# Residual and result kept channel-major outside a two-layer DiT backbone kernel, in place of transposes on TensorE

## The chip, the cores and the metric

One core of one Trainium2 chip runs the whole program. The metric is the device time of one execution in microseconds, as a median over runs.

## What is computed

A backbone of two layers works on 512 latent tokens `x` with 256 context tokens `ctx` ahead of them, each token with 1024 channels. Layer 0 mixes tokens by windowed attention, layer 1 by a gated linear recurrence (HGRN2). A channel mixer (ConvGLU) closes each layer. Every sub-layer normalises its input, scales and shifts it by vectors made from the conditioning, and adds its output, times a gate, to the stream. Cut to what matters here:

```python
for layer in range(DEPTH):                     # 2
    hx = rms_norm(x, norm1_g[layer]) * (1.0 + sc1) + sh1
    hc = rms_norm(ctx, norm1_g[layer]) * (1.0 + csc1) + csh1
    yx, yc = windowed_gqa(hx, hc, ...) if layer == 0 else hgrn2_bidir(hx, hc, ...)
    x = x + g1 * yx                            # the residual
    x = x + g2 * conv_glu(rms_norm(x, norm2_g[layer]) * (1.0 + sc2) + sh2, ...)
    if not last:
        ctx = ctx + cg1 * yc                   # and the same for the context
        ctx = ctx + cg2 * conv_glu(...)
return x                                       # (1, 512, 1024)
```

`x` has a batch of one and comes as 512 rows of 1024 channels; the result has the same form.

## The kernel before, in words

Everything inside the kernel is channel-major. The 1024 channels are 8 blocks (`d`) of 128 channels, a block lies on the 128 partitions, and tokens run along the free dimension. The stream is held as `self.xl` (128 x 8 x 512, latent) and `self.xc` (128 x 8 x 256, context). A matrix product takes weights (128 x 128) as the stationary operand and tokens as the moving one. Weights and activations are split into a high and a low fp32r part; each product is three (`wh` with high, `wh` with low, `wl` with high). ScalarE makes `wh` and VectorE `wl` (L118 and L119 in `load_w`) from the raw tile `wr` or `wd` that a transfer from the SP queue brought.

Outside, tokens are rows, so the kernel turns the data round at three places:

- `first_norm` loads `x` and `ctx` token-major (SP queue, at the start), normalises and transposes them for the first sub-layer. It keeps no copy of the raw stream.
- `attn_out` (L928 to L951) is the output projection of the attention. For each of four pairs `(dp, dp+4)` of channel blocks it loads the weights, and for each block of a pair it loads the stream's slice again, token-major, into `xs` by two transfers on ScalarE's queue (L937: 4 x 128 tokens of `x`, 256 KB; L938: 2 x 128 of `ctx`, 128 KB). Six transposes of 128 x 128 on TensorE (L941) put it into a PSUM tile `xT`, and two ScalarE copies (L943) move it to `xl` and `xc`. Then 48 products (8 input blocks, three parts, latent and context) fill the PSUM tile `ao`, and `add_gated` (VectorE, L955) adds `ao` times the gate to `xl` and `xc`. Behind each pair stand the squares of the new stream (`square_acc`, L552 and L554) and the operands `hs` of the channel mixer (`combos`, L382 to L404, L449 to L452). Two PSUM pools serve `xT` and two serve `ao`, in turn.
- `done1` (L1536 to L1556) is called for each channel block when its last down projection (`dn`, L177) has been added to the stream (L1116; L1111 for the last block, which is added in two halves of 256 tokens). It transposes the block back (L1551, four transposes into the PSUM tile `xo`; L1543, two for each half of the last block), copies `xo` to an SBUF tile `ost` or `osl` on ScalarE (L1552, L1544) and starts a transfer on the SP queue: one for each of three pairs of blocks (L1556, 512 KB), one for block 6 (L1554, 256 KB) and one for each half of block 7 (L1545, 128 KB).

The attention ends with `split_o`: the output `o` of the last group of heads, copied from the PSUM tile `pv` (L884), is split into `oh`, its high part by ScalarE (L893), its low one by VectorE (L894). `oh` is the moving operand of the output projection; its last two input blocks come from this last split.

The order of the instructions on each engine is set by a scheduler that simulates a timeline; weight loads and splits have a raised priority. An edit in one place can therefore move rows that it does not name.

Of the kernel before, what the change touches and what calls it, by code (L numbers as in the profile page):

```python
# [8 lines left out]
F32 = mybir.dt.float32  # L9
F32R = mybir.dt.float32r  # L10
BF16 = mybir.dt.bfloat16
AF = mybir.ActivationFunctionType
ALU = mybir.AluOpType
AX = mybir.AxisListType
PSUM = bass.MemoryType.PSUM

P = 128
D = 1024
KT = D // P
LAT = 512  # L20
CTX = 256
TOK = LAT + CTX
NQ = LAT // P
# [50 lines left out]
class Kernel:  # L74
    def __init__(self, tc, a, dbg=None):
        self.tc, self.nc, self.a, self.dbg = tc, tc.nc, a, dbg or {}
# [848 lines left out]
        es.close()  # L925
        return ohs[0]

    def attn_out(self, oh, hs, acc, tmp, pj, pp):  # L928
        nc, a = self.nc, self.a
        wout = a["attn_w_out"][0]  # L930
        for dp in range(KT // 2):
            w = self.load_w([self.wcols(wout, d * P, P) for d in (dp, dp + 4)])
            for j in range(2):
                d = dp + 4 * j
                xs = tmp.tile([P, 6, P], F32, tag="xs", name="xs")
                cs = slice(d * P, (d + 1) * P)
                nc.scalar.dma_start(out=xs[:, 0:4], in_=a["x"][0, :, cs].rearrange("(t p) c -> p t c", p=P))  # L937
                nc.scalar.dma_start(out=xs[:, 4:6], in_=a["ctx"][0, :, cs].rearrange("(t p) c -> p t c", p=P))  # L938
                pt = pp.tile([P, 1024], F32, tag="p2", name="xT")
                for i in range(6):  # L940
                    nc.tensor.transpose(pt[:, i * P:(i + 1) * P], xs[:, i], self.ident)  # L941
                for lo, hi, x in self.segs(False):
                    nc.scalar.activation(x[:, d], pt[:, lo:hi], AF.Copy)  # L943
                ps = pj.tile([P, 1024], F32, tag="pj", name="ao")
                self.mm_feat(w[j], KT, lambda k: (oh[:, 0, k], oh[:, 1, k]), self.spans(ps, FULL))
                self.add_gated(0, 2, d, ps, False)
            ops = self.combos(self.halves(0, 1, dp, 386, False, tmp, ("G", "nt")), dp, hs)
            for _ in range(2):
                next(ops)
            for d in (dp, dp + 4):  # L950
                self.square_acc(d, acc, False, tmp, first=(d == 0))  # L951
# [477 lines left out]
    def run(self, stop=99):  # L1429
        nc, a = self.nc, self.a  # L1430
# [10 lines left out]
        oh = self.attention(hn)  # L1441
# [17 lines left out]
        tmp = self.pool(es, "tmpA", 1)  # L1459
        acp = self.pool(es, "accA", 1)  # L1460
        acc = Rp.tile([P, TOK], F32, tag="acc", name="acc0")
        hs = [*(h1[:, i] for i in range(4)), h2[:, 0], h2[:, 1]]
        with ExitStack() as e2:
            pp, pj = (_Turn([self.pool(e2, f"{n}{i}", 1, PSUM) for i in range(2)]) for n in ("ppA", "pjA"))
            xsp = self.pool(e2, "xsp", 2)
            self.attn_out(oh, hs, acc, _Multi(tmp, xsp, ("xs",)), pj, pp)
        rs.close()
        if stop == 2:
            self.dump_x(); es.close(); hss.close(); hB.close(); top.close(); return
# [7 lines left out]
        gp = self.pool(es, "gpA", 5)  # L1477
# [27 lines left out]
        e2 = ExitStack()  # L1505
        sc = self.pool(e2, "sc", 2, PSUM)
        lv = self.pool(e2, "lv", 2, PSUM)
        pj = self.pool(e2, "pj", 2, PSUM)
        part = self.hgrn(hn2[0], R, accs[0], hb, pj, lv, sc)
# [3 lines left out]
        hs = [hs1[:, i] for i in range(8)]  # L1513
        ot = self.pool(es, "ot", 1)
        acc = Rp.tile([P, LAT], F32, tag="acc", name="acc2")
# [10 lines left out]
        tmp = self.pool(es, "tmpB", 2)  # L1526
        acp = self.pool(es, "accB", 1)
        gp = self.pool(es, "gpB", 9)
# [2 lines left out]
        bk = [self.pool(es, "bkB0", 4, PSUM), self.pool(es, "bkB1", 4, PSUM)]  # L1531
        bk = _Turn(bk, bk[:1] * 3)
        rows = self.row_factor(acc, True, tmp, bk, "ps", 512, R, -1.0)
        ost = {}

        def done1(d, bank, part=None):  # L1536

            if d == KT - 1:
                n = LAT // 2
                pt = bank("xo")  # L1540
                o = gp.tile([P, 2, P], F32, tag="g", name="osl")
                for i in range(2):
                    nc.tensor.transpose(pt[:, i * P:(i + 1) * P], self.xl[:, d, part * n + i * P:part * n + (i + 1) * P], self.ident)  # L1543
                nc.scalar.activation(o, pt[:, :n].rearrange("p (i c) -> p i c", c=P), AF.Copy)  # L1544
                nc.sync.dma_start(out=a["out"][0, part * n:part * n + n, d * P:(d + 1) * P].rearrange("(t p) c -> p t c", p=P), in_=o)  # L1545
                return
            if d % 2 == 0:
                ost[0] = gp.tile([P, NQ, 256], F32, tag="g", name="ost")
            pt = bank("xo")
            for i in range(NQ):  # L1550
                nc.tensor.transpose(pt[:, i * P:(i + 1) * P], self.xl[:, d, i * P:(i + 1) * P], self.ident)  # L1551
            nc.scalar.activation(ost[0][:, :, (d % 2) * P:(d % 2) * P + P], pt[:, :LAT].rearrange("p (i c) -> p i c", c=P), AF.Copy)  # L1552
            if d == KT - 2:
                nc.sync.dma_start(out=a["out"][0, :, d * P:(d + 1) * P].rearrange("(t p) c -> p t c", p=P), in_=ost[0][:, :, 0:P])  # L1554
            elif d % 2:
                nc.sync.dma_start(out=a["out"][0, :, (d - 1) * P:(d + 1) * P].rearrange("(t p) c -> p t c", p=P), in_=ost[0])  # L1556

        self.ffn(1, hs, R, rows, True, tmp, acp, bk, gp, done1)
        es.close()
        rs.close()  # L1560
# [8 lines left out]
class _Halves:  # L1569
# [5 lines left out]
    def tile(self, *a, **kw):  # L1575
        return self.parts.pop(0)
# [12 lines left out]
        return self.pools[-1].tile(*a, **kw)  # L1589


class _Multi:


    def __init__(self, p0, p1, tags):
        self.p0, self.p1, self.tags = p0, p1, tags

    def tile(self, shape, dt, tag=None, name=None, **kw):
        return (self.p1 if tag in self.tags else self.p0).tile(shape, dt, tag=tag, name=name, **kw)


_INS = ['x', 'c', 'ctx', 'c_ctx', 'ada_w', 'ada_b', 'norm1_g', 'norm2_g', 'attn_w_in', 'attn_w_out', 'attn_q_gain',
        'attn_k_gain', 'attn_sink', 'hgrn_w_in', 'hgrn_w_out', 'hgrn_o_gain', 'hgrn_lb_logits', 'ffn_w_up',
        'ffn_conv_w', 'ffn_conv_b', 'ffn_w_down']
# [18 lines left out]
```

## Time and profile before

| | before |
|---|---|
| median of 3 runs | 1773.47 us (1773.41 to 1774.19) |
| the profiled execution's own time | 1773.3 us |
| its span in the trace | 1771.5 us |
| granted TensorE clock, mean | 0.999 |
| TensorE busy | 1742.6 us, 98% of the span |
| VectorE, ScalarE, GpSimd busy | 1308.5, 833.6, 247.3 us |
| moved by DMA | 166.44 MB, mean 94 GB/s |

The span is the stretch between the first and the last record of the execution; its own time is the 1.8 us longer device time. Busy times of one engine count its instructions that overlap only once. The chain that the page shows is followed back from the last instruction: each piece is work, or a wait for what released it. TensorE (PE) overlaps the load of one weight tile (PEld) with the product before it.

### The profile page before, as it was taken

The numbers are of one execution on the slowest core, as the hardware profiler recorded it, in microseconds if no ns is written. First come the engines' busy times: TensorE is split into PE (matmuls) and PEld (weight loads), VectorE is DVE, ScalarE is ACT, GpSimd is POOL, SyncE is SP. The second block draws the span as 40 slices with busy tenths as digits, with TensorE's granted clock in tenths as the row PEclk, the third lists the DMA queues.
The fourth block names the chain that finished last, engine by engine and source line by source line (L and its number), as shares of the span: only waits on it lengthen the run. The fifth ranks groups of instructions, "written<-read, shape, count | busy, mean of one in ns | idle before, by whom it ended". The sixth has DMA issues, their size and how long they took to land.

```text
span 1771.5 us, 32299 instructions
## 1 busy us (share of the span) xinstructions
PE 1742.6 (98%) x13033; PEld 1528.3 (86%) x13033; DVE 1308.5 (74%) x2394; ACT 833.6 (47%) x1740; POOL 247.3 (14%) x232
## 2 busy tenths in 40 slices
PE   5999999999999999999999999999999999999998
PEld 4967775789889888999999889999897899999997
DVE  6576677477777776867867767777776699999984
ACT  4355556565534443534455333333333465565553
POOL 1133333200100110100100101111110001111110
PEclk9999999999999999999999999999999999999999
DMA  9351005133333343213114212121225423333311
GB/s 309 110 198 42 24 2 191 52 92 113 122 120 99 123 139 96 87 42 99 54 52 117 62 45 61 53 57 40 58 73 190 123 72 105 110 105 108 91 59 66
DMA packets 205188, 166.44 MB, mean 94 GB/s; under 512 B 5406, under 2 KB 199023, under 8 KB 199919
## 3 DMA queue, kind: packets, MB, share of 16 engines
q1 hardware_dynamic: 197376, 160.47, 29.5%
q10 hardware_dynamic: 7662, 3.92, 0.8%
q8 instruction: 102, 1.67, 0.4%
q14 instruction: 48, 0.39, 0.1%
HBM read 162.27 MB, written 2.10 MB: 93 GB/s over the span
## 4 chain that ended last, share of the span: by engine, by line
PE 96%; DMA 2%; DVE 1%; ACT 0%; issue 0%; POOL 0%; SPq 0%; ACTq 0%; DVEq 0%
PE dn L177 17%; PE pZ L195 17%; PE pV L195 8%; PE pf L177 8%; PE pY L195 4%; PE pjq L634 4%; PE pv L177 4%; PE ao L177 4%; PE pv L882 3%; PE pgate L177 3%; PE pq L177 3%; PE pt L872 3%; PE ada L316 2%; PE kv L634 2%; PE pd L969 2%; PE S L814 2%
## 5 line engine op out<-in xcount | busy, mean ns | idle before, releaser
L195 PE MATMUL pZ<-hs,wh 128*128 128x386 f32 (+1 forms) x1312 | 296.7, 314 | 0.0
L177 PE MATMUL dn<-g,wh 128*128 128x512 f32 (+1 forms) x1062 | 268.0, 356 | 0.0
L142 ACT ACTIVATE wh<-wr 128x512 fp32r<-128x512 f32 x246 | 153.7, 629 | 242.7 <-PE pZ L195 89.2
L118 ACT ACTIVATE wh<-wr 128x512 fp32r<-128x512 f32 (+2 forms) x204 | 120.2, 603 | 271.5 <-PE pf L177 82.1
L195 PEld LDWEIGHTS pZ<-hs,wh 128*128 128x128 f32 x1312 | 224.1, 189 | 14.8 <-ACT wh L142 5.9
L143 DVE TENSOR_TENSOR wl<-wr,wh 128x512 fp32r<-128x512 f32 x246 | 182.5, 746 | 35.8 <-ACT wh L142 31.6
L195 PE MATMUL pZ<-hs,wl 128*128 128x386 f32 (+1 forms) x656 | 204.7, 313 | 0.0
L177 PEld LDWEIGHTS dn<-g,wh 128*128 128x128 f32 x1062 | 174.7, 189 | 25.7 <-ACT g L1062 0.3
L119 DVE TENSOR_TENSOR wl<-wr,wh 128x512 fp32r<-128x512 f32 (+2 forms) x204 | 140.4, 695 | 74.3 <-ACT wh L118 65.1
L992 POOL TENSOR_TENSOR gg<-gg,R 128x772 f32<-128x772 f32 (+1 forms) x41 | 85.3, 2079 | 715.2 <-DVE gg L991 626.0
L177 PE MATMUL dn<-g,wl 128*128 128x512 f32 (+1 forms) x531 | 162.1, 355 | 0.0
L195 PE MATMUL pV<-hs,wh 128*128 128x386 f32 (+1 forms) x656 | 148.6, 313 | 0.0
L195 PEld LDWEIGHTS pZ<-hs,wl 128*128 128x128 f32 x656 | 123.4, 188 | 0.1
L177 PE MATMUL pf<-hn,wh 128*128 128x512 f32 (+1 forms) x512 | 117.7, 344 | 0.6 <-DVE gate L1160 0.6
L195 PEld LDWEIGHTS pV<-hs,wh 128*128 128x128 f32 x656 | 111.9, 189 | 1.3 <-issue 0.8
L195 PE MATMUL pV<-hs,wl 128*128 128x386 f32 (+1 forms) x328 | 102.2, 313 | 0.0
L177 PEld LDWEIGHTS dn<-g,wl 128*128 128x128 f32 x531 | 89.4, 188 | 14.2
L1116 DVE SCALAR_TENSOR_TENSOR xl<-dn,mod,xl 128x512 f32<-128x512 f32 x95 | 70.5, 745 | 29.6 <-PE dn L177 29.5
L177 PEld LDWEIGHTS pf<-hn,wh 128*128 128x128 f32 x512 | 79.4, 189 | 12.1 <-DVE gate L1160 0.8
L634 PE MATMUL pjq<-wh,hn 128*128 128x256 f32 x384 | 76.8, 289 | 0.0
L195 PE MATMUL pY<-hs,wh 128*128 128x386 f32 (+1 forms) x328 | 76.7, 314 | 0.0
L822 POOL TENSOR_SCALAR P<-P,r 128x512 f32<-128x512 f32 (+1 forms) x64 | 53.0, 832 | 95.8 <-DVE r L821 73.8
(321 smaller groups left out, 3895.9 us busy)
## 6 DMA issues: line engine op xcount, KB each, us to landing
wr<-in_ffn_w_up SPq DMA_DIRECT2D x88, 512.0 KB, 5.2
wada<-in_ada_w SPq DMA_DIRECT2D x40, 1024.0 KB, 5.0
wr<-in_hgrn_w_in SPq DMA_DIRECT2D x40, 512.0 KB, 5.1
ar<-in_ada_w SPq DMA_DIRECT2D x32, 256.0 KB, 7.0
wd<-in_ffn_w_down SPq DMA_DIRECT2D x16, 512.0 KB, 3.4
wr<-in_attn_w_in SPq DMA_DIRECT2D x6, 1024.0 KB, 8.5
wr<-in_ffn_w_down SPq DMA_DIRECT2D x12, 384.0 KB, 3.0
wr<-in_attn_w_out SPq DMA_DIRECT2D x8, 512.0 KB, 4.3
```

Source lines behind the costliest of these rows:

```text
L118: nc.scalar.activation(wh, src, AF.Copy)
L119: nc.vector.tensor_tensor(wl, src, f(wh), op=ALU.subtract)
L142: nc.scalar.activation(ops[i][0], src, AF.Copy)
L143: nc.vector.tensor_tensor(ops[i][1], src, f(ops[i][0]), op=ALU.subtract)
L177: nc.tensor.matmul(o, lhsT=wt, rhs=at[:, t0:t0 + o.shape[1]], start=(first and n == 0 and i == 0), stop=(last and n == len(ks) - 1 and i = ...
L195: self.nc.tensor.matmul(ps, lhsT=wt, rhs=at, start=(first and k == 0 and i == 0), stop=(k == nk - 1 and i == 2), skip_group_check=not first)
L634: nc.tensor.matmul(out, lhsT=x, rhs=y[:, wk], start=(start and k == 0 and j == 0), stop=(stop and k == KT - 1 and j == 2))
L822: nc.gpsimd.tensor_scalar(p[:, :n], p[:, :n], r[:, j:j + 1], 1.0, op0=ALU.mult, op1=ALU.mult)
L872: nc.tensor.transpose(pt[:, j * P:(j + 1) * P], pr[j][:, b * P:(b + 1) * P], self.ident)
L882: nc.tensor.matmul(pv[a * HD:(a + 1) * HD, 0:256], lhsT=V[:, tiles[b], g, :], rhs=pT[:, a * 256:(a + 1) * 256], start=(b == 0), stop=(b == ...
L992: times = lambda eng, o, x, y: eng.tensor_tensor(o, x, y, op=ALU.mult)
L1116: nc.vector.scalar_tensor_tensor(x[:, d], o, self.modc(l, v, 5, d), x[:, d], op0=ALU.mult, op1=ALU.add)
```

## The change

The host hands over the stream a second time, as `xT` (1024 x 512) and `ctxT` (1024 x 256), and takes the result as `out_0` of 1024 x 512, which it transposes back. In `attn_out` the transfers go straight to `self.xl` and `self.xc`, one of each per pair of blocks: four of 512 KB and four of 256 KB on ScalarE's queue (L934 after), with rows of 2 KB and 1 KB. The transposes, their PSUM tiles, the copies and `xs` are gone, and the PSUM banks that served them go to `ao`: four pools, `p0 p1 p2 p3 p2 p3 p2 p3` in turn over the eight blocks. `done1` is one transfer from `xl` for each block (L1531 after): seven of 256 KB, and two of 128 KB for the last block. `first_norm` is as before.

```diff
-    def attn_out(self, oh, hs, acc, tmp, pj, pp):
+    def attn_out(self, oh, hs, acc, tmp, pj):
...
             w = self.load_w([self.wcols(wout, d * P, P) for d in (dp, dp + 4)])
+            for x, src in ((self.xl, a["xT"]), (self.xc, a["ctxT"])):
+                nc.scalar.dma_start(out=x.rearrange("p (j d) t -> p j d t", j=2)[:, :, dp],
+                                    in_=src.rearrange("(j d p) t -> p j d t", j=2, p=P)[:, :, dp])
             for j in range(2):
                 d = dp + 4 * j
-                xs = tmp.tile([P, 6, P], F32, tag="xs", name="xs")
-                cs = slice(d * P, (d + 1) * P)
-                nc.scalar.dma_start(out=xs[:, 0:4], in_=a["x"][0, :, cs].rearrange("(t p) c -> p t c", p=P))
-                nc.scalar.dma_start(out=xs[:, 4:6], in_=a["ctx"][0, :, cs].rearrange("(t p) c -> p t c", p=P))
-                pt = pp.tile([P, 1024], F32, tag="p2", name="xT")
-                for i in range(6):
-                    nc.tensor.transpose(pt[:, i * P:(i + 1) * P], xs[:, i], self.ident)
-                for lo, hi, x in self.segs(False):
-                    nc.scalar.activation(x[:, d], pt[:, lo:hi], AF.Copy)
                 ps = pj.tile([P, 1024], F32, tag="pj", name="ao")
...
-            pp, pj = (_Turn([self.pool(e2, f"{n}{i}", 1, PSUM) for i in range(2)]) for n in ("ppA", "pjA"))
-            xsp = self.pool(e2, "xsp", 2)
-            self.attn_out(oh, hs, acc, _Multi(tmp, xsp, ("xs",)), pj, pp)
+            pj = [self.pool(e2, f"pjA{i}", 1, PSUM) for i in range(4)]
+            self.attn_out(oh, hs, acc, tmp, _Turn(pj + 2 * pj[2:]))
...
-            if d == KT - 1:
...
-                for i in range(2):
-                    nc.tensor.transpose(pt[:, i * P:(i + 1) * P], self.xl[:, d, part * n + i * P:part * n + (i + 1) * P], self.ident)
-                nc.scalar.activation(o, pt[:, :n].rearrange("p (i c) -> p i c", c=P), AF.Copy)
-                nc.sync.dma_start(out=a["out"][0, part * n:part * n + n, d * P:(d + 1) * P].rearrange("(t p) c -> p t c", p=P), in_=o)
-                return
...
-            for i in range(NQ):
-                nc.tensor.transpose(pt[:, i * P:(i + 1) * P], self.xl[:, d, i * P:(i + 1) * P], self.ident)
-            nc.scalar.activation(ost[0][:, :, (d % 2) * P:(d % 2) * P + P], pt[:, :LAT].rearrange("p (i c) -> p i c", c=P), AF.Copy)
...
+            c = slice(0, LAT) if part is None else slice(part * LAT // 2, (part + 1) * LAT // 2)
+            nc.sync.dma_start(out=a["out"][d * P:(d + 1) * P, c], in_=self.xl[:, d, c])
...
+    data["xT"] = np.ascontiguousarray(data["x"][0].T)
+    data["ctxT"] = np.ascontiguousarray(data["ctx"][0].T)
...
-    args["out"] = nc.dram_tensor("out_0", (1, LAT, D), F32, kind="ExternalOutput").ap()
+    args["out"] = nc.dram_tensor("out_0", (D, LAT), F32, kind="ExternalOutput").ap()
...
-    return r.results[0]["out_0"]
+    return np.ascontiguousarray(r.results[0]["out_0"].T)[None]
```

The scheduler's order differs at the end of the attention and in the tail behind the last up projection; elsewhere the engines' rows stand as before. (Numbers behind a name tell buffers apart and differ between the two programs; `oh_3949`, `xl_4232` and `xc_4250` are the same in both.)

TensorE where the attention's last value products `pv` meet the output projection, before:

```order
L177 MATMUL ao_4304<-oh_3949,wl_4281 128x512
L177 MATMUL ao_4304<-oh_3949,wl_4281 128x256
L882 MATMUL pv_4191<-pT_4197,V_917 64x256 x2
L941 MATMUL xT_4358<-cst_64,xs_4355 128x128 x4
L882 MATMUL pv_4191<-pT_4204,V_917 64x256 x2
L941 MATMUL xT_4358<-cst_64,xs_4355 128x128 x2
L177 MATMUL ao_4367<-oh_3949,wh_4284 128x512
```

The same place after:

```order
L177 MATMUL ao_4342<-oh_3949,wh_4281 128x512
L882 MATMUL pv_4191<-pT_4197,V_917 64x256 x2
L177 MATMUL ao_4342<-oh_3949,wh_4281 128x256
L882 MATMUL pv_4191<-pT_4204,V_917 64x256 x2
L177 MATMUL ao_4342<-oh_3949,wh_4281 128x512
L177 MATMUL ao_4342<-oh_3949,wh_4281 128x256
```

Where two transposes stood behind the last `pv`, 16 more products of the block `ao_4342` follow, and 15 of the block `ao_4496`, ahead of the first product that takes the last two input blocks of `oh`.

ScalarE behind the last copy of `o`, before (`y` of L383 are small norm factors):

```order
L884 ACTIVATE o_918<-pv_4191 128x2x128
L383 ACTIVATE y_4418<-mod0_123 128x2
L383 ACTIVATE y_4423<-mod0_123 128x2
L937 DMA xs_4531<-in_x 128x4x128
L893 ACTIVATE oh_3949<-o_918 128x768 x2
L938 DMA xs_4531<-in_ctx 128x2x128
L118 ACTIVATE wh_4452<-wr_4449 128x512
L118 ACTIVATE wh_4456<-wr_4449 128x512
L943 ACTIVATE xl_4232<-xT_4295 128x512
L943 ACTIVATE xc_4250<-xT_4295 128x256
```

After:

```order
L884 ACTIVATE o_918<-pv_4191 128x2x128
L934 DMA xc_4250<-in_ctxT 128x2x256
L118 ACTIVATE wh_4439<-wr_4424 128x512
L893 ACTIVATE oh_3949<-o_918 128x768 x2
L383 ACTIVATE y_4393<-mod0_123 128x2
L383 ACTIVATE y_4398<-mod0_123 128x2
L934 DMA xc_4250<-in_ctxT 128x2x256 x3
L118 ACTIVATE wh_4427<-wr_4424 128x512
L118 ACTIVATE wh_4431<-wr_4424 128x512
L934 DMA xl_4232<-in_xT 128x2x512 x4
L118 ACTIVATE wh_4583<-wr_4580 128x512
L382 ACTIVATE y_4393<-xl_4232,gs0_125 128x512
```

One weight split stands ahead of the `oh` splits now, the `xc` transfers around them, and the four `xl` transfers behind two more weight splits, where the copies from `xT` stood.

TensorE in the tail, at the first use of the last channel-mixer block `g` (`g_19318` before, `g_19226` after), before:

```order
L177 MATMUL dn_19446<-g_18944,wl_19439 128x512
L177 MATMUL dn_19446<-g_19131,wh_19438 128x512 x2
L177 MATMUL dn_19446<-g_19131,wl_19439 128x512
L177 MATMUL dn_19407<-g_19318,wh_19399 128x512
L177 MATMUL dn_19408<-g_19318,wh_19403 128x512
```

After:

```order
L177 MATMUL dn_19383<-g_18852,wl_19379 128x512
L177 MATMUL dn_19383<-g_19039,wh_19378 128x512 x2
L177 MATMUL dn_19383<-g_19039,wl_19379 128x512
L177 MATMUL dn_19416<-g_18852,wh_19408 128x512 x2
L177 MATMUL dn_19315<-g_19226,wh_19307 128x512
L177 MATMUL dn_19316<-g_19226,wh_19311 128x512
```

Ahead of that use TensorE has 27 `dn` products behind its last up product before, and 47 after; `dn_19383` is the sixth block of the last round, `dn_19446` was the third.

More of the change, by code (lines that the diff above doesn't have):

```diff
@@ L1533, in run @@
         rows = self.row_factor(acc, True, tmp, bk, "ps", 512, R, -1.0)
-        ost = {}
         def done1(d, bank, part=None):
-            if d == KT - 1:
-                n = LAT // 2
-                pt = bank("xo")
-                o = gp.tile([P, 2, P], F32, tag="g", name="osl")
-                for i in range(2):
-                    nc.tensor.transpose(pt[:, i * P:(i + 1) * P], self.xl[:, d, part * n + i * P:part * n + (i + 1) * P], self.ident)
-                nc.scalar.activation(o, pt[:, :n].rearrange("p (i c) -> p i c", c=P), AF.Copy)
-                nc.sync.dma_start(out=a["out"][0, part * n:part * n + n, d * P:(d + 1) * P].rearrange("(t p) c -> p t c", p=P), in_=o)
-                return
-            if d % 2 == 0:
-                ost[0] = gp.tile([P, NQ, 256], F32, tag="g", name="ost")
-            pt = bank("xo")
-            for i in range(NQ):
[L1551 to L1556, printed above, removed]
+            c = slice(0, LAT) if part is None else slice(part * LAT // 2, (part + 1) * LAT // 2)
+            nc.sync.dma_start(out=a["out"][d * P:(d + 1) * P, c], in_=self.xl[:, d, c])
         self.ffn(1, hs, R, rows, True, tmp, acp, bk, gp, done1)
@@ L1589, in tile @@
         return self.pools[-1].tile(*a, **kw)
[L1592 to L1599, printed above, removed]
 _INS = ['x', 'c', 'ctx', 'c_ctx', 'ada_w', 'ada_b', 'norm1_g', 'norm2_g', 'attn_w_in', 'attn_w_out', 'attn_q_gain',
```

## The prediction

> **What bounds the kernel now.** I read the page first, its busy shares and its chain by engine, then the chain piece by piece in the two stretches that the change touches, then the timeline of the other engines there.
>
> ```profile
> span 1771.5 us, 32299 instructions
> ...
> PE 1742.6 (98%) x13033; PEld 1528.3 (86%) x13033; DVE 1308.5 (74%) x2394; ACT 833.6 (47%) x1740; POOL 247.3 (14%) x232
> ...
> PE 96%; DMA 2%; DVE 1%; ACT 0%; issue 0%; POOL 0%; SPq 0%; ACTq 0%; DVEq 0%
> ```
>
> TensorE (PE) is busy 98% of the span and carries 96% of the chain that ended last. An edit that takes PE work away therefore gains that work's length, if nothing else becomes late. The profiled execution took 1773.3 us, 1.8 more than its span; the median of the three runs is 1773.47, so 0.2 is added to a time reckoned from the profile.
>
> The first stretch, the end of the attention with its output projection, in the windows view (length, then busy time of PE, weight loads, DVE, ACT and GpSimd, the granted clock, DMA share, GB/s), and PE's transposes there:
>
> ```profile
> 328.50:408.90 80.40, 80.28 (x489) 68.02 (x492) 49.13 (x93) 48.35 (x114) 2.70 (x16) 1.00 0.27 79
> ```
>
> ```profile
> L941 PE MATMUL xT<-cst,xs 128*128 128x128 f32 x48 | 6.8, 275 | 0.0
> ```
>
> PE has no idle time (80.28 of 80.40), DVE and ACT are busy for 61%, and the clock is at 1.00 with all 48 transposes inside. In the chain over 328 to 412 us (start, length, piece) the same transposes stand so:
>
> ```profile
> by line: PE ao L177 80.5%; DMA wr<-in_ffn_w_up 6.4%; PE xT L941 6.2%; PE pv L882 5.2%; PE pt L872 3.8%; ACT o L884 0.5%; SPq L96 0.4%; issue 0.2%; PE Sc L814 0.1%; PE Sc L817 0.1%
> ...
> 332.45 0.66 PE xT L941 x6
> ...
> 342.01 0.59 PE xT L941 x4
> 342.60 0.61 PE pv L882 x4
> 343.21 0.02 issue
> 343.23 0.39 ACT o L884
> 343.62 0.04 issue
> 343.67 10.76 PE ao L177 x60
> 354.43 0.87 PE xT L941 x8
> ...
> 400.44 8.44 PE ao L177 x48
> ```
>
> 6.2% of 84 us is 5.2 us of transposes on the path. Between 343.21 and 343.67 PE also waits 0.46 us for ScalarE to copy out the last attention output o. Then only projection products follow, 48 for each block of 128 channels, 0.176 us each.
>
> The second stretch is the tail, the chain over 1749 to 1772 us:
>
> ```profile
> by line: PE dn L177 59.5%; PE xo L1551 13.9%; ACT ost L1552 2.6%; ACTq L1619 1.2%; ACT osl L1544 1.2%; issue 0.1%
> ...
> 1752.12 0.57 PE xo L1551 x4
> ...
> 1765.37 0.45 PE xo L1551 x4
> 1765.82 0.02 issue
> 1765.85 0.60 ACT ost L1552
> 1766.44 0.28 ACT osl L1544
> 1766.72 0.28 ACTq L1619
> ```
>
> The xo transposes take 13.9% of 23 us, 3.2 us in seven groups; the last group (0.45) stands behind the last down product, the other six (2.75) stand between products. Behind the last product, at 1765.37, the timeline has:
>
> ```profile
> 1765.41 0.48 DVE L1111 SCALAR_TENSOR_TENSOR xl<-dn,mod,xl 128x256 f32<-128x256 f32 x1 [0.58 <-PE dn L177]
> ```
>
> ```profile
> 1767.19 0.92 SPq L1545 DMA_DIRECT2D out<-osl  x2
> ```
>
> The last add is done at 1765.89, but the last of two output transfers is issued only around 1767.65 (its half of the 0.92), after transposes and copies. From there to the span's end are 1771.5 - 1767.65 = 3.85 us.
>
> **Part 1, the residual loads.** Removed: 48 transposes on PE, 5.2 us, all on the path; the ACT copies (16, of 0.4 to 0.6 us) and half of the 16 ACT-queue transfers were beside PE, worth nothing. In the new order PE has 31 ao products between the last pv and the first that needs the last channel pair of oh (16 of one block, 15 of the next). They take 31 x 0.176 = 5.5 us and have to cover the chain that makes oh:
>
> ```profile
> 344.89 1.83 DVE L894 TENSOR_TENSOR oh<-o,oh 128x768 fp32r<-128x768 f32 x2 [1.23 <-ACT oh L893]
> ```
>
> ```profile
> 346.75 1.15 ACT L118 ACTIVATE wh<-wr 128x512 fp32r<-128x512 f32 x2 [1.16 <-DVE oh L894]
> 347.81 0.58 ACT L943 ACTIVATE xl<-xT 128x512 f32<-128x512 f32 x1
> ```
>
> Before, oh is complete at 344.89 + 1.83 = 346.72, 3.5 us after the last pv. One weight split (half of 1.15) is moved ahead of it, so about 4.1 us against 5.5 of cover: the wait of 0.46 for o goes and no new one comes, with 1.4 us to spare. If that cover were gone the price is 4.1 less what is left of 5.5. Against this, the new order cuts the last pv products apart with ao rows. Such a switch costs about 0.15: four xT beside pv took 0.59, where half of the eight in 0.87 is 0.44. Three more switches cost 0.45. Net: 5.2 + 0.46 - 0.45 = **-5.2 us**.
>
> The loads come late, and that is where this part could fail. The four xl transfers stand on ScalarE behind two weight splits that end, by the rows above, about where ScalarE used to copy xl (347.8). What can be said of their landing:
>
> ```profile
> wr<-in_attn_w_in SPq DMA_DIRECT2D x6, 1024.0 KB, 8.5
> ...
> xs<-in_x ACTq DMA_DIRECT2D x8, 256.0 KB, 2.9
> out<-ost SPq DMA_DIRECT2D x3, 512.0 KB, 2.9
> ```
>
> The new 512 KB ones lie between 2.9 and 8.5. The nearest row is 2.9 (same queue or same size), but with 3.1 MB in one burst at 79/0.27 = 293 GB/s (10.7 us for all) I take 5 for the first. The first reader is DVE's gated add:
>
> ```profile
> 351.17 0.75 DVE L955 SCALAR_TENSOR_TENSOR xl<-ao,mod,xl 128x512 f32<-128x512 f32 x1 [0.51 <-PE ao L177]
> ```
>
> So DVE is held until about 353, 2 us (0 to 5) longer than before. Queued behind it on DVE are the weight splits of later blocks, on ScalarE the norm steps that read xl. PE needs neither soon. The first two blocks have PSUM banks that no later block of this stage takes (four pools, before two), so the first bank wanted again is the third block's, two blocks (2 x 8.44 us) after that block's end, and the split weights held up behind the add are those of the third pair of channels, about 20 us on. The delay costs 0; with a landing at 8.5 and one block of cover (8.44) it would cost next to nothing still.
>
> **Part 2, the output.** Removed between products: six xo groups, **-2.75 us**. A further wait goes in the tail:
>
> ```profile
> PEld dn L177 <- ACT g L1062: 0.3, 1, 0.3
> ```
>
> Before, PE ran 27 products between its last up product and the first that needs the last g; the new order has 47, 20 x 0.23 = 4.6 us more cover, so this small wait goes: **-0.2** (0 to 0.5). Behind the last product: before 1767.65 - 1765.37 = 2.28 us to the last issue; now the add alone (0.04 + 0.48) and about 0.15 to the issue, 0.67: **-1.6 us**. Last, the transfers: nine instead of six, all in the last six microseconds of products; 2.1 MB at 293 GB/s are 7.2 us, of which some 5.6 lie beside the products and the rest inside the 3.85 of the last transfer. I take **+0.2** (0 to +1.5).
>
> The sum is -5.2 - 2.75 - 0.2 - 1.6 + 0.2 = -9.6: 1773.3 - 9.6 = 1763.7 for the profiled execution, 1763.9 as a median.
>
> Two rules of the Trainium skill speak to these terms. Six transposes cost 0.66 us of path here, 0.11 each, though each lasts 275 ns by its own row. "TensorE: Matmul & The Clock Gate", Part 4, puts one 128x128 transpose at about 275 ns in a kernel's context and says that the full clock does not engage in transpose mode; by that, 80 of them would be 22 us. The trace agrees with the length of one, not with the sum, and shows the clock at 1.00 around them. "DMA: Bandwidth & Descriptors", Rules for kernel authors, says to coalesce small transfers, since each pays a fixed part (about 2.0 us in Anatomy of one DMA); by that, the three more transfers would cost up to 6 us, and the time would be an estimated 1769.9. Both mechanisms stand among the rivals, priced by rows.
>
> **The rivals.**
>
> *Output transfers pay their whole length in part* (chance 0.08). Each of the last few waits for engines still busy with earlier ones. For: 2.1 MB go out in a burst. Against: at 293 GB/s a 256 KB transfer needs 0.9 us of the 2.9 that it takes to land, so neighbours fit in. Worth +1.5: 1765.4.
>
> *The attention's gain is given back at the entry of the channel mixer* (0.07). After the last ao product the chain goes through a load of up weights (6.4% of 84 us, 5.4). If that load or the norm steps on ACT and DVE, not PE, set the entry, PE arrives earlier and waits. Against: that load is issued at the end of the ao products, and moves with them; DVE and ACT have 39% to spare. Then only the tail's 4.4 remains: 1768.9, 1769.1 as a median.
>
> *No change* (0.04): this, and a late xl load that stops PE for 4 to 5 us, where the scheduler's covers of 15 us fail.
>
> *Slower: the output transfers go one behind another* (0.02). The first is issued about 5.6 us before the last product ends; nine of 2.9 us end 26.1 us later, 20.5 after the last product, where I have 4.5: 1763.9 + 16 = 1779.9. It decides from about 2.2 us per transfer ((4.5 + 9.6 + 5.6)/9). Against: the rate above, 0.9 of the 2.9 in motion.
>
> *Transposes cost their whole 275 ns* (0.02): 80 x 0.275 = 22.0 in place of the 5.2 + 3.2 counted; 1763.9 - 13.6 = 1750.3. Against: six in 0.66, eight in 0.87.
>
> That the change does not do what it says is excluded: no xT or xo row is left in the order of PE.
>
> **How the numbers follow.** The forecast has 0.77. The predicted time is its own, 1763.9. The range takes in the open ends of its terms: upward 1.3 of the transfers and half of the attention's gain (2.6) given back, 1767.8; downward the switches (0.45), the rest of the g wait (0.3) and gaps that PE's fewer switches may save in both stretches (some 14 groups by 0.15, 2.1), 1761.0. It leaves out the give-back case, the slower one and the full transpose price. A measurement of this kernel tells about 0.2% (3.5 us) from no change. Faster by over that needs less than 1769.9: the forecast, the first two rivals and the last, 0.94; within it 0.04; slower 0.02.
>
> **What would show it.** In the profile after, the output projection should be PE ao pieces end to end, some 5 us shorter, with no PE wait on xl, xc or oh; a DVE wait on an xl transfer of 1 to 5 us at its first add without PE behind it; the tail without groups between products; the last add followed by the last transfer within 0.7 us, and about 4 us to the end. The prediction is wrong if PE waits for oh, xl or up weights in the attention's end for over 2 us, or if the end lies over 6 us behind the last product.

## The result, and the profile after

The changed kernel takes 1762.2 us (median of 4, 1761.77 to 1764.35) against 1773.66 of the kernel before (4 runs): ratio of the two 0.9937, 95% interval 0.9925 to 0.995, 11.5 us less. The forecast was 1763.9 in a range of 1761.0 to 1767.8. The profiled execution took 1761.99. Its page begins:

```profile
span 1760.1 us, 32119 instructions
...
PE 1732.5 (98%) x12953; PEld 1519.9 (86%) x12953; DVE 1308.2 (74%) x2394; ACT 823.7 (47%) x1715; POOL 247.4 (14%) x232
```

The span is 11.4 us shorter and PE's busy time 10.1, with the same share: the bound is the same and has less work. The chain over 326 to 404 us, from the attention's last scores to the end of the output projection (start, length, piece):

```profile
327.78 0.12 PE Sc L814
...
343.67 0.58 PE pv L882 x4
344.25 0.31 PE ao L177
344.56 0.58 PE pv L882 x4
345.15 57.77 PE ao L177 x328
402.91 0.02 issue
```

Behind the last `pv` stand 328 products without one break: no transposes, no wait for o, none for the stream's loads. The same last score product was at 328.34 before, and the projection ended at 408.88 (chain of before, 0.02 of issue ahead of the up weights' load):

```profile
328.34 0.12 PE Sc L814
```

The tail's chain after:

```profile
1736.94 1.43 PE pZ L195 x12
1738.38 18.67 PE dn L177 x90
1757.04 0.03 issue
1757.07 0.48 DVE xl L1105
```

And where the last up product ended before:

```profile
1742.21 1.43 PE pZ L195 x12
1743.64 6.59 PE dn L177 x28
```

From these rows comes the ledger of the two profiled executions:

| stretch | before | after | change | forecast |
|---|---|---|---|---|
| start to the last scores | 328.34 | 327.78 | -0.56 | 0 |
| to the end of the projection | 80.54 | 75.13 | -5.41 | -5.2 |
| to the end of the last up product | 1334.76 | 1335.47 | +0.71 | 0 |
| to the end of the last down product | 21.73 | 18.66 | -3.07 | -2.95 |
| behind it, to the span's end | 6.13 | 3.06 | -3.07 | -1.4 |
| sum | 1771.5 | 1760.1 | -11.4 | -9.6 |

The first row is not the change's: nothing differs there, and in the other runs this stretch took 327.58 to 329.92 us. Two rows are as forecast, one is twice as large, one was not forecast.

The first gated add, on DVE (in brackets its idle time before it, and what ended that), and the output's transfers on SP's queue:

```profile
353.73 0.75 DVE L949 SCALAR_TENSOR_TENSOR xl<-ao,mod,xl 128x512 f32<-128x512 f32 x1 [2.73 <-PE ao L177]
```

```profile
1751.40 6.51 SPq L1531 DMA_DIRECT2D out<-xl  x9
```

The add waited for its block, not for the load, which landed (its data had arrived) 4.6 us after its issue at 349.04, just ahead of the add. In `e1`, which runs the same instructions here, the load took 5.8 us, and the add waited 4.0 for it. The nine issues end at 1757.91, 0.36 behind the last add; from there 2.19 us remain.

### The profile page after: what moved, and what is told of

Same layout as the page of the kernel before. It is cut to its first block, busy times and chain, and to the rows that moved or that the text cites. A ratio compares the mean times of both kernels' runs of the same rounds, so it can differ in the third digit from the quotient of the medians.

```text
span 1760.1 us, 32119 instructions
## 1 busy us (share of the span) xinstructions
PE 1732.5 (98%) x12953; PEld 1519.9 (86%) x12953; DVE 1308.2 (74%) x2394; ACT 823.7 (47%) x1715; POOL 247.4 (14%) x232
## 4 chain that ended last, share of the span: by engine, by line
PE 96%; DMA 2%; DVE 1%; ACT 0%; issue 0%; SPq 0%; POOL 0%; DVEq 0%; ACTq 0%
PE dn L177 17%; PE pZ L195 17%; PE pV L195 8%; PE pf L177 8%; PE pY L195 4%; PE pjq L634 4%; PE pv L177 4%; PE ao L177 4%; PE pv L882 3%; PE pgate L177 3%; PE pq L177 3%; PE pt L872 3%; PE ada L316 2%; PE kv L634 2%; PE ho L177 2%; PE pd L963 2%
```

## The experiments

**Each half alone.** `e1` takes the changed kernel and puts the old output back; `e2` takes the kernel before with the new output.

```diff
 e1, against the changed kernel:
-            nc.sync.dma_start(out=a["out"][d * P:(d + 1) * P, c], in_=self.xl[:, d, c])
+                nc.tensor.transpose(pt[:, i * P:(i + 1) * P], self.xl[:, d, i * P:(i + 1) * P], self.ident)
...
 e2, against the kernel before:
-                nc.tensor.transpose(pt[:, i * P:(i + 1) * P], self.xl[:, d, i * P:(i + 1) * P], self.ident)
...
+            nc.sync.dma_start(out=a["out"][d * P:(d + 1) * P, c], in_=self.xl[:, d, c])
```

> Only the residual loads are changed (and the PSUM pools of the projection with them); the result leaves through the 32 transposes, copies and six transfers as before. Theory (path work: the transposes, and the wait for o, were on PE's path, nothing gives them back): 5.2 to 6.0 us under the kernel before, about 1767.8, with the output projection's end some 5.5 us earlier and the tail as long as before (21.7 us from the last up product to the last down product, 6.1 behind it). Rival (given back at the entry of the channel mixer or by another order there): 0 to 2 us under it. If both halves do not add up to the whole change (11.4), one of them only pays with the other.

> Only the output is changed; the residual comes through the 48 transposes as before. Theory: 3.1 us less between the last up product and the last down product, and 3.1 less behind it, so 6.1 under the kernel before, about 1767.2. Rival (the tail's gain depends on a slack that the earlier part made): 4.4 us or less under it, as forecast in the first place.

Measured: e1 1768.29 (ratio 0.9974, 0.9962 to 0.9985), 5.5 under the kernel before, measured beside it (1773.82); e2 1767.39 (0.9963, 0.995 to 0.9975), 6.4 under it. Together 12.0, against 11.5 for both at once, inside the intervals: the halves add up. The chain of e1's tail, and of e2's:

```profile
1759.03 2.12 PE dn L177 x18
1761.15 0.45 PE xo L1545 x4
1761.60 0.02 issue
1761.63 0.60 ACT ost L1546
```

```profile
1742.89 18.67 PE dn L177 x90
1761.56 0.03 issue
1761.58 0.48 DVE xl L1111
```

e1 spends 5.55 us behind the last product (its span is 1766.7) where the kernel before had 6.13, with the same instructions. So two profiles of one tail differ by 0.6 there. e2's product stretch is 18.67 as in the changed kernel, and 3.44 remain behind it (span 1765.0).

**Why so little is left behind the last product.** `e3` sends the same nine transfers in pieces of 512 bytes, `e4` the last block in one transfer, `e7` the first six blocks in pairs, `e8` the very last transfer from another queue.

```diff
 e3: -  nc.sync.dma_start(out=a["out"][d * P:(d + 1) * P, c], in_=self.xl[:, d, c])
     +  o = a["out"].rearrange("(t x) l -> t (x l)", x=2)[c, d * P:(d + 1) * P]
     +  nc.sync.dma_start(out=o.rearrange("(t p) i -> p t i", p=P), in_=self.xl[:, d, c].rearrange("p (t i) -> p t i", i=P))
 e4: +  if part == 0:
     +      return
     +  c = slice(0, LAT)
 e7: +  if part is not None or d == KT - 2:
            nc.sync.dma_start(out=a["out"][d * P:(d + 1) * P, c], in_=self.xl[:, d, c])
     +  elif d % 2:
     +      nc.sync.dma_start(out=a["out"][(d - 1) * P:(d + 1) * P].rearrange("(j p) t -> p j t", p=P), in_=self.xl[:, d - 1:d + 1])
 e8: -  nc.sync.dma_start(out=a["out"][d * P:(d + 1) * P, c], in_=self.xl[:, d, c])
     +  q = nc.scalar if part == 1 else nc.sync
     +  q.dma_start(out=a["out"][d * P:(d + 1) * P, c], in_=self.xl[:, d, c])
```

> The changed kernel with the same nine transfers of the same sizes, but their pieces in memory are 512 bytes (128 tokens) at a stride of 4 KB, as the result before had them for single blocks, in place of rows of 2 KB and 1 KB; so the result stands in the wrong places. It asks why 3.06 us are left behind the last add and issue where 4.5 were forecast. Theory A (the longer rows make the last transfers short): the end moves back by 1.0 to 1.5 us, to about 4.3 behind the last product, 1761.5 for the span. Theory B (it is the amount still queued at the end that counts, and fewer bytes are): within 0.3 us of the changed kernel.

> The changed kernel with the last block's two transfers of 128 KB as one of 256 KB behind the last add. Theory A (the rows' length counts): 128 KB more at the end cost some 0.35 us at 380 GB/s and one issue of 0.37 is saved: 0 to 0.3 us longer. Theory B (bytes queued at the end count): 0.7 us or more longer.

> The changed kernel with the first six blocks of the result sent in three transfers of 512 KB in place of six of 256 KB; six in all, as before the change. If the number of transfers costs (a fixed part for each, in turn): 2 us or more under the changed kernel, with the end some 2 us nearer to the last product. My theory (they overlap, and only the last one's own length counts): within 0.5 us of it, if anything later, since a pair waits for its second block.

> The changed kernel with the very last transfer of 128 KB issued by ScalarE in place of SyncE, so that it is not behind the issue of the first half. If the issue in turn (0.4 to 0.5 us each) sets the end: 0.3 to 0.5 us under the changed kernel in the span behind the last product (3.1 to 3.4 there now). If the transfer alone does: no change.

The output's transfers in the changed kernel, and in e3 (size, median us to landing):

```profile
out<-xl SPq DMA_DIRECT2D x7, 256.0 KB, 2.1
out<-xl SPq DMA_DIRECT2D x2, 128.0 KB, 1.7
```

```profile
out<-xl SPq DMA_DIRECT2D x7, 256.0 KB, 2.6
out<-xl SPq DMA_DIRECT2D x2, 128.0 KB, 2.8
```

With 512-byte pieces a 128 KB transfer lands after 2.8 us and not 1.7 (1.7 to 1.9 in e2, e5, e6, e9 and e10, which send it in 1 KB rows too), and 3.90 us remain behind the last product (span 1760.7, product end at 1756.80) where 3.06 did; the median is 1763.75. Theory A is right in the sign, with 0.84 of the 1.0 to 1.5 that it expected; against the longest end of a run with the changed output left as it is (3.44, e2) it is 0.46. But e3 does not tell the two theories apart. The short pieces slow the whole burst, from 379 GB/s in the changed kernel to 285 over 1754 to 1756 us, and over 1758 to 1759 the DMA engines are still 96% busy where they were 63%. So more is queued ahead of the last transfer too, and which of the two makes it late is not shown. e4 leaves 3.49 (median 1762.78), between what the two theories gave, so it tells nothing apart. e7 leaves 3.60 (1763.35): six transfers are no better than nine, if anything later, and no fixed part in turn is paid for each. e8 leaves 3.15 (1762.68), no less than the changed kernel. The issue in turn costs nothing there: in the changed kernel the first half's issue is over at 1757.34, and the last add ends at 1757.55, so SyncE was free for the second.

**What the four banks do.** The change moved PSUM banks too, from the transposes to the projection. `e5` gives the projection two, as before.

```diff
-            pj = [self.pool(e2, f"pjA{i}", 1, PSUM) for i in range(4)]
-            self.attn_out(oh, hs, acc, tmp, _Turn(pj + 2 * pj[2:]))
+            pj = [self.pool(e2, f"pjA{i}", 1, PSUM) for i in range(2)]
+            self.attn_out(oh, hs, acc, tmp, _Turn(pj))
```

> The changed kernel, but the projection has only two PSUM banks, as before the change, so the bank of one block is wanted again one block later. Theory (the stream's loads land in time, and the adds free a bank within one block of 8.4 us): as long as the changed kernel, 1762.2 within 1 us, and no wait of PE between the blocks. Rival (the four banks are what keeps a late load or add from PE): PE waits at the second or third block, 2 us or more, 1764 or above.

Measured 1767.81 (ratio 0.9965, 0.9951 to 0.9979): the theory that I held falls. The chain of e5 in the projection, and its waits there (us in total, times, longest):

```profile
347.73 1.84 DVE oh L894 x2
349.57 0.02 issue
349.59 0.01 ACT wh L118
349.60 5.48 DMA xl<-in_xT
355.08 0.02 issue
355.11 0.75 DVE xl L949
355.86 0.40 DVE xc L949
356.26 0.14 issue
356.39 52.09 PE ao L177 x288
```

```profile
PE ao L177 <- DVE xc L949: 3.5, 1, 3.5
...
DVE xl L949 <- DMA xl<-in_xT: 1.8, 1, 1.8
```

The load of `xl` starts only when the last split of `oh` has read `o`. ScalarE, which issues it, stands still for that split ahead of the two weight splits that come before the load:

```profile
349.59 0.63 ACT L118 ACTIVATE wh<-wr 128x512 fp32r<-128x512 f32 x1 [0.97 <-DVE oh L894]
```

In the built program the wait for the split of `oh` is on the first of these weight splits, the load has none of its own, and both write where the attention's tiles were. The load lands 5.5 us later, the add follows, and the third block, whose bank the first block held, waits with PE standing still for 3.5 us. The projection then takes longer still: from the end of the last `pv` to its end 62.8 us, where 57.8 is usual. Of these 5.0 us, 3.5 are the wait and 1.4 are in the products: 288 in 52.09, where 0.176 each give 50.7. The windows view shows why (length, PE busy, then the other engines; the last three columns are granted clock, DMA share, GB/s), first of e5, then of `e9`, a run without the pause that is described below:

```profile
340.00:352.00 12.00, 12.00 (x72) 9.51 (x69) 4.26 (x11) 4.91 (x11) 0.26 (x6) 1.00 0.37 101
352.00:357.00 5.00, 1.52 (x8) 1.09 (x7) 2.58 (x5) 2.28 (x4) 0.00 (x0) 0.89 0.89 299
357.00:362.00 5.00, 5.00 (x25) 4.36 (x24) 3.72 (x8) 4.79 (x13) 0.00 (x0) 0.77 0.99 297
362.00:370.00 8.00, 8.00 (x48) 7.01 (x47) 5.82 (x12) 4.83 (x12) 0.10 (x1) 1.00 0.03 8
```

```profile
352.00:357.00 5.00, 5.00 (x31) 4.35 (x30) 0.94 (x2) 1.27 (x2) 0.00 (x0) 1.00 0.99 350
357.00:362.00 5.00, 5.00 (x30) 4.39 (x29) 4.20 (x9) 4.46 (x10) 0.00 (x0) 1.00 0.84 246
```

Behind the pause the granted clock of e5 is 0.77 in the mean of 5 us. In a finer window it is 0.50 throughout; before 355.8 and from 359.4 on it is 1.00:

```profile
355.85:359.25 3.40, 2.85 (x9) 2.50 (x10) 3.40 (x9) 3.36 (x8) 0.00 (x0) 0.50 1.06 366
```

The products resume at 356.39, so they run for 2.86 us at half the clock. That loses 1.43 us, the whole of the 1.4. The DMA traffic is not the cause: e9 moves as much in these windows, at a clock of 1.00 and at full pace. The Trainium skill, "TensorE: Matmul & The Clock Gate", Part 1, says that an idle window of about 3.4 us brings the throttle back; the trace agrees roughly, with a clock that fell some 2.9 us into a pause of 3.48 us.

`e9` gives the third block a bank of its own: three banks, the first for the first block alone, `_Turn(pj[:1] + 4 * pj[1:])`.

> The changed kernel with three PSUM banks for the projection, the first for the first block alone and the other two in turn. With two banks (previous run) PE stood for 3.5 us at the third block, until the first block's add had freed its bank, and that add stood until the stream's first transfer had landed. New theory (a bank held by the late load is the whole of it but for the shorter cover of oh): the third block has a bank of its own, so that wait goes; what stays is at most 1 us at oh, since the order has 16 products there and not 31: 1762.2 to 1763.5. Rival (fewer banks cost by something else, the order or the blocks' sequence): 1766 or above, as with two.

Measured 1761.64 (ratio 0.9934, 0.992 to 0.9948), 12.8 under the kernel before, measured beside it (1774.39). The chain of e9, and its first add:

```profile
345.26 0.58 PE pv L882 x4
345.84 57.77 PE ao L177 x328
```

```profile
356.76 0.75 DVE L949 SCALAR_TENSOR_TENSOR xl<-ao,mod,xl 128x512 f32<-128x512 f32 x1 [3.36 <-DMA xl<-in_xT]
```

The add waits 3.4 us for the load here, longer than in e5, and PE does not notice: 57.77 us for the 328 products, as in the changed kernel. TensorE's order from the last `pv` to the third block is the same in e5 and e9 (in the built programs). So it is the bank held by the late add, and nothing else of having fewer banks. Not even the wait of up to 1 us at `oh` came; 16 products suffice as its cover.

**What the transposes alone cost.** `e6` puts 48 transposes of a constant beside the two banks of e5, `e10` beside the three of e9, into banks that nobody reads (two in e6, one in e10). The diff is e10's.

```diff
+                pt = pp.tile([P, 1024], F32, tag="pj", name="xT")
+                for i in range(6):
+                    nc.tensor.transpose(pt[:, i * P:(i + 1) * P], self.ident, self.ident)
                 ps = pj.tile([P, 1024], F32, tag="pj", name="ao")
```

> The changed kernel with two PSUM banks for the projection and 48 transposes of a constant beside it, six for each block, into two other banks that nobody reads; loads straight to the stream as in the changed kernel. So only TensorE's work of the transposes comes back, without their loads, copies or waits. Theory (they cost what the chain shows, 0.11 us each when several follow one another): 5.2 us more than with two banks alone, 1767.4 or so. Rival (the gain lay in the waits and the order, since transposes of a wait-free constant run between products): 0 to 2 us more. Second rival (each costs its whole 275 ns): 13 us more.

> The same three banks, and 48 transposes of a constant, six for each block, into the fourth bank, read by nobody. Theory (a transposition beside others costs 0.11 us of path, whatever waits for it): 8 x 0.66 = 5.2 us more than with three banks alone, less what of the first six fills the wait for oh (up to 0.7): 4.5 to 5.2. Rival (the transposes only filled waits, so the gain came from the loads and the order): under 2 us.

e6: 1768.64, only 0.8 above e5. By itself that reads like the first rival; but e6 has no pause. By its chain 62 products and 12 transposes stand between its last `pv` and the third block, where e5 has 40 products, so e6 compares two different bounds. e10 has a base without a pause: 1767.09 against 1761.64, 5.45 us for 48 transposes. The intervals of these two medians just touch, so the size rests on the profiles: from the last scores to the end of the projection e10 takes 80.35 us and e9 75.14, 5.21 more. The chain of e10:

```profile
374.64 8.40 PE ao L177 x48
383.05 0.66 PE xT L940 x6
383.70 8.43 PE ao L177 x48
392.13 0.66 PE xT L940 x6
```

The transposes depend on nothing and are waited for by nothing, and each six still put 0.66 us between the products. The second rival (275 ns each, 13 us) is out.

## Why the prediction was right, point by point

**The 48 transposes, -5.2: right.** The stretch lost 5.41 in the profile, e1 is 5.5 faster as a whole, and e10 prices the transposes alone at 5.45, or 5.21 in the stretch itself. (Where the prediction says that only projection products follow behind 343.67, its own rows show most of the transposes between them; its sum has them.)

**The cover of `oh`: right.** The wait of 0.46 for o is gone and no other came; even 16 products, not 31, cover the chain (e9).

**The late loads, cost 0: right, but one sentence of the reason was wrong.** I put DVE's add off to about 353, by 2 us (0 to 5); it came at 353.73 and its releaser was PE. That is one execution: over the ten runs with these loads, the changed kernel among them, the first landed 4.1 to 7.0 us after its issue (5 had been put), and the add stood for it, 4.0 us in e1 and 3.4 in e9 (there at 356.76). PE was free of it in all three, since the first blocks' banks were not wanted again. But I also wrote that one block of cover "would cost next to nothing still". With two banks it costs 5.0 us (e5, at a landing of 5.5), nearly the whole gain of this part. I had set the landing (8.5) against the length of a block (8.44), as if the add came due a block after the load's start. But the scheduler runs the first two blocks ahead, into the attention's end, so only 40 of their products (7.0 us) are left behind the last `pv`, while the load cannot start until 3.9 us behind it. The cover is reckoned from where the transfer may start to where the bank is wanted.

**Between the products of the tail, -2.75 and -0.2: right.** -3.07 together, the same in e2.

**Behind the last product, -1.4: mis-sized.** It was -3.07 in the two profiles. The end of the old tail is 5.55 in e1 and 6.13 in the kernel before; the new one lies between 3.03 and 3.44 in the six runs that leave it as changed (the changed kernel, e2, e5, e6, e9, e10). The step that failed is the last one of the sum: I carried over the 3.85 from the last issue to the end and added 0.2 for a burst of more transfers. The last issue itself came as forecast, 0.53 behind the last product (0.67 in the sum), but from there to the end it was 2.53 and not 4.05. In the same measure e1 has 3.5 and e3 3.4, both with 512-byte pieces in the last transfers like the kernel before, and the six runs have 2.5 to 2.9. So the end goes with the row length, by 0.5 to 0.9 from those six to e3. The rest, up to some 0.5 between e3 and the kernel before, I cannot assign; it is about what two profiles of the same tail differ by.

**What I had not forecast: +0.71 in the 1335 us between.** Most of it stands at one place, the entry of the HGRN output projection, where PE waits for a modulation vector that VectorE adds behind a weight split, which waits for a load. Before, and after:

```profile
PE ho L177 <- DVE mod L331: 1.0, 1, 1.0
```

```profile
PE ho L177 <- DVE mod L331: 1.6, 1, 1.6
```

The wait is 0.8 in e2, 0.9 in e9, 1.0 in e8 and 1.3 to 1.5 in e1, e3, e4, e5, e7 and e10. But e3, e4, e7 and e8 run the changed kernel's own instructions up to the output, and their stretch is 1335.43, 1335.09, 1335.03 and 1334.67 us, the last one shorter than the 1334.76 of the kernel before. So the row moves by as much from one execution to the next, and it is not shown that the change costs anything there. What sets the wait stays open.

**The rivals.** Transfers that pay their length in part or one behind another: no (e7, e8, and 3.06 us at the end). The prediction's 2.0 us for each transfer come from the Trainium skill, "DMA: Bandwidth & Descriptors", Anatomy of one DMA, which gives them for transfers that GpSimd issues; the output's are issued by SyncE. The attention's gain given back at the entry of the channel mixer: no, e1 keeps 5.5 of it. Transposes at their full 275 ns: no (e10). The direction came by the mechanism that was named. Of the 1.7 us by which the profiled execution (1761.99) lies under the forecast sum (1763.7), the end gave 1.7, the start 0.6, the two stretches of products 0.3, and the loss between took 0.7 back (the last 0.2 is rounding and what lies around the span). That the start and the stretch between nearly cancel is chance.

No version tried here is clearly faster than the changed kernel: e9 at 0.9934 and the changed kernel at 0.9937 lie inside each other's intervals.

## What to carry to other kernels

On an engine that was busy all the time, a short instruction cost the gap that it made between its neighbours in the chain (0.11 us for a transpose that lasts 275 ns), and it gave that back when it went, whether or not anything waited for it. When a copy is replaced by a transfer into a long-lived tile, ask what lay in that memory before (here the attention's tiles, in use until the last split of its output, which delays the start), and how long the accumulator's bank is held by whoever waits for the transfer: of the two banks set free by the removed work, one was worth nearly as much as the work (5.0 and 5.4 us). And the shape of rows in memory counted at the kernel's end, where nothing hides the last transfer.

## What the runs showed of the hardware that I had not expected

A pause of TensorE of 3.48 us cost 1.4 us more than itself: the granted clock fell to 0.50 some 2.9 us into the pause and stayed there for 3.4 us (e5). And a 128 KB store to memory landed 1.7 us after its issue in rows of 1 KB, 2.8 in pieces of 512 bytes, at the end of bursts of the same 2.1 MB that moved at 379 and 285 GB/s (the changed kernel and e3).
